# A planned order of instructions: forced first loads, slack ahead of the array, and local repacking

## The chip, the cores and the metric

The kernel runs on one core of a Trainium2 chip. The metric is the device time of one execution in microseconds (us); the kernel before takes 576.88 us, the median of three runs (576.75 to 577.52). Six queues issue instructions side by side and wait for each other by semaphores: PE (TensorE, the matmul array, with PEld for the loading of its weights), DVE (VectorE), ACT (ScalarE), POOL (GpSimd) and SP (SyncE, which here only starts DMAs).

## The reference

Two layers over x of 512 tokens by 1024 channels in float32. In each layer one projection `x @ w_in` (1024 by 3352) feeds three mixers side by side; the gated results go through one output projection and a LayerNorm.

```python
proj = x @ w_in
(rq, rk, rv, rg, nq, nkc, nvc, nks, nvs, nkw, nvw, ng, ngl, lx, lg) = jnp.split(proj, ...)
y_ret = retention(rq, rk, rv) * silu(rg)                    # 4 heads of 64, chunks of 128 tokens
y_nsa = nsa(nq, nkc, nvc, nks, nvs, nkw, nvw, ngl) * silu(ng)  # 8 heads; compressed, selected, window branch
y_lru = rg_lru(lx) * silu(lg)                               # convolution of width 4, gated scan
x = layer_norm(alpha * x + concat(y_ret, y_nsa, y_lru) @ w_out)
```

The NSA part makes softmax probabilities P for each tile of 128 tokens, group of 4 heads and branch, scales each by a gate over its sum, transposes them on PE and multiplies them with the values.

## The kernel before, in words

**Arithmetic.** Every product on PE keeps float32 accuracy by a split: an operand is written as a high part (`XH`, `wh`, `pth`) and a low part (`XL`, `wl`, `ptl`), and a product is three matmuls, high by high, high by low, low by high. ACT makes the high parts by a copy, DVE or POOL the low parts by a subtraction. So each weight that arrives by DMA in a raw buffer `wr` passes ACT (`wh`) and POOL or DVE (`wl`) before PE reads it, and each activation passes ACT (`XH`) and DVE (`XL`).

**Staging.** The activations stand as eight tiles of 128 channels by 512 tokens, `XH[:, k]`, `XL[:, k]`. The weights come in chunks of up to 280 columns, each in two halves of four k-tiles, by the function `weights` (line 563). There are two raw buffers `wr` and four buffers each of `wh` and `wl`. The order of the chunks is fixed: `nv` (the values and gates of NSA, 280 columns), `nk` (its keys, 256), `nq0`, `cmp`, `nq1`, and so on. In the first chunk of the first layer the loads are cut into single k-tiles, 140 KB of weights and 256 KB of x each, and x is loaded beside it (`load_x`, line 597; its buffer is `Y`). `proj_n` (line 611) has tokens as rows of the output, 3 matmuls of 280 columns for each k and token tile; `proj_t` (line 602) has 128 columns of the projection as rows and 512 tokens as columns. PSUM has banks A (three), S (two), M, T and O: `A` takes projections, `S` scores, `T` transposes, `O` the attention output.

**What sets the order.** Nothing is issued while the Python code runs. Every operation goes through `record` (line 201) into a `Plan` (line 287) with its engine, a cost in ns by formula (`Engine.cost`, line 244), and what it reads and writes. That is why all rows of the profile have one line, L208, or L239 for one group of matmuls (`together`, line 235); rows are told apart by the names of their tiles. `Plan.schedule` (line 353) then does list scheduling: `forward` (line 373) goes through model time and at each step issues, of the operations whose inputs are ready, the one that can start first, ties by priority. `lag` (line 348) is the model's delay from an operation to one that waits for it; rotating buffers are given out in recorded order. The first priorities are the longest remaining path plus noise from a random generator (`SEED`). `backward` schedules from the end, and up to six rounds of backward and forward keep the plan with the smallest model end. `emit` issues that plan; each engine then runs its instructions in that fixed order and only waits on semaphores. For the first chunk two of the weight loads are issued on ACT's queue (`W_ACT = 2`), the rest on SP's.

**The end.** `out_mm` and `out_norm` (lines 1087 and 1095) do the output projection in four chunks of 256 columns and the LayerNorm; at the end of layer 0 the four token tiles of `R` are normalised on DVE and POOL, transposed on PE through `T` (`T<-idr,R`, half a row of channels at a time) and split into the next layer's `XH` and `XL`.

Of the kernel before, what the change touches and what calls it, by code (L numbers as in the profile page):

```python
# [78 lines left out]
def _constants():  # L79
# [12 lines left out]
    for i in range(NT):  # L92
# [15 lines left out]
           ACT=dict(PE=281, DVE=152, ACT=148, POOL=170), POOL=dict(PE=203, DVE=60, ACT=75, POOL=100))  # L108
# [3 lines left out]
COLD = 6827.0  # L112
TURN = 130.0
GRAIN = 8
DMA_RATE = 360.0
BANKS = dict(A=3, M=1, S=2, T=1, O=1)
PBUFS = 7
WARM = 9
W_ACT = 2

NORM = [["AG", "AG", "VV", "VV"], ["AG", "AG", "VV", "VV"]]
LOCKS = True
HELD = 115.0
ACT_SOME = 0.0
POOL_EARLY = 60.0
K_ORDER = [0, 1, 6, 7, 2, 3, 4, 5]
# [3 lines left out]
SCALE = "GGGV"  # L130
W_ENG = "GGGG"
W_CUT = 2
SEED = 12
NOISE = 300.0
B_ATT = 50e3
B_LRU = 0.0
B_RET = 0.0
# [56 lines left out]
class Engine:  # L194
# [40 lines left out]
    def together(self, *products):  # L235

        def call():
            for out, lhsT, rhs, kw in products:
                self.queue.matmul(out.view(), lhsT.view(), rhs.view(), **kw)  # L239

        cost = 110.0 * len(products)
        self.plan.add(self.name, call, cost, [r for x in products for r in x[1:3]], [x[0] for x in products], None, False)

    def cost(self, what, args, kw):
        at = lambda x: x.view(0) if isinstance(x, Ref) else x
        size = lambda x: int(np.prod(x.shape[1:]))
        in_psum = lambda x: x.space == PSUM
        row = lambda x: x.offset // x.ap[0][0]
        out = at(args[0])
        n = size(out)  # L250
        if self.name == "SP":
            return max(475.0, out.nbytes() / DMA_RATE)
        if what == "dma_start":
            return 475.0
        if self.name == "PE":
            if what == "transpose":
                return 0.87 * at(args[1]).shape[0]
            m = size(at(args[1]))
            if at(args[2]).dtype == F32R:
                return max(0.4465 * n + 4.0, 0.86 * m)  # L260
            return max(1.8 * n, 1.73 * m)
        src = [at(x) for x in args[1:] if isinstance(x, Ref)]
        psum = any(in_psum(x) for x in src)
        moved = any(row(x) != row(out) for x in src)
        if self.name == "ACT":
            aps = any(isinstance(kw.get(k), Ref) for k in ("bias", "scale"))
            some = psum and src[0].shape[0] < P
            return (52 if psum else 93) + 0.833 * n + 93 * aps + 93 * ("accum_out" in kw) + 16 * moved + ACT_SOME * some
        n = max([n] + [size(x) for x in src])
        if self.name == "POOL":  # L270
            if kw.get("op") == ALU.pow:
                return 268 + 243.0 * n
            if what == "memset":
                return 60 + 0.5 * n
            return 230 + 0.863 * n if what == "tensor_scalar" else 120 + 2.2 * n
        if what == "reciprocal":
            return 60 + 6.3 * n
        if what == "tensor_tensor_scan":
            return 2.21 * n
        if what == "tensor_scalar" and "accum_out" in kw:  # L280
            return 190 + 1.042 * n
        if what in ("tensor_copy", "tensor_scalar", "memset") and not psum and not in_psum(out):
            return 67 + 0.521 * n + 62 * (len(src) - 1) + 93 * moved
        return 70 + 1.042 * n + 93 * moved + (8 if what == "tensor_tensor_reduce" else 0)


class Plan:
    ENGINES = ("PE", "DVE", "ACT", "POOL", "SP")

    def __init__(self, nc):  # L290
        self.ops, self.cells, self.bias = [], {}, 0.0
        queues = (nc.tensor, nc.vector, nc.scalar, nc.gpsimd, nc.sync)
        self.engines = [Engine(self, e, q) for e, q in zip(self.ENGINES, queues)]

# [15 lines left out]
        return self.cells[key]  # L310

    def add(self, eng, call, cost, reads, writes, table, lock, dma=False):
        op = Op(eng, call, cost, table, lock and LOCKS, len(self.ops))
        op.dma = dma
        for r in reads:
            q, m = self.touched(r)
            op.after.update(o for o, q2, m2 in r.buf.writes if q & q2 and m & m2)
        for r in writes:
            q, m = self.touched(r)
            op.after.update(o for o, q2, m2 in r.buf.writes + r.buf.reads if q & q2 and m & m2)  # L320
        for r in reads:
            r.buf.reads.append((op, *self.touched(r)))
        for r in writes:
            b, (q, m) = r.buf, self.touched(r)
            b.writes = [w for w in b.writes if w[1] & ~q or w[2] & ~m] + [(op, q, m)]
            b.reads = [w for w in b.reads if w[0] is op or w[1] & ~q or w[2] & ~m]
        op.after.discard(op)
        op.bufs = {r.buf for r in reads + writes}

        op.rows = {}  # L330
        if eng in ("ACT", "DVE") and not dma:
            for kind, refs in (("W", writes[:1]), ("R", reads)):
                for r in refs:
                    ap = r.view(0)
                    op.rows.setdefault((kind, ap.space == PSUM), ap.offset // ap.ap[0][0])
        for b in op.bufs:
            b.users += 1
        for o in op.after:
            o.before.append(op)
        op.bias = self.bias  # L340
        self.ops.append(op)
# [5 lines left out]
    @staticmethod  # L347
    def lag(a, b):
        if a.dma:
            return LAG_DMA  # L350
        return LAG[a.eng].get(b.eng, 150.0)

    def schedule(self):

        rank, noise = {}, NOISE * np.random.RandomState(SEED).standard_normal(len(self.ops))
        for op in reversed(self.ops):
            rank[op] = op.cost + max((self.lag(op, o) + rank[o] for o in op.before), default=0.0)
        self.end = self.forward({op: noise[op.ix] - rank[op] - op.bias for op in self.ops})
        best = self.end, {op: op.start for op in self.ops}
        for _ in range(ROUNDS):  # L360
            self.end = self.forward(self.backward())
            if self.end < best[0]:
                best = self.end, {op: op.start for op in self.ops}
        if best[0] < self.end:
            self.end = self.forward(best[1])
        return self.end

    @staticmethod
    def held(op, rows):
# [3 lines left out]
    def forward(self, prio):  # L373
# [16 lines left out]
        def place(op):  # L390
# [7 lines left out]
                t = max([t] + [end + TURN for e, end in b.seen.items() if e != op.eng])  # L398
            return t

        while len(self.order) < len(self.ops):
            best = None
            for e in ("POOL", "PE", "DVE", "ACT", "SP"):
                pick = None
                for op in ready[e]:
                    at = place(op)
                    if at is None:
                        continue
                    t = max(op.known, at, free[e] + self.held(op, rows), ports[e] if op.lock else 0.0)
                    k = (t, prio[op], op.ix)  # L410
                    if pick is None or k < pick[0]:
                        pick = k, op
                if pick and (best is None or pick[0][0] < best[0][0]):
                    best = pick
# [18 lines left out]
                ports["POOL"] = op.end  # L433
            ready[op.eng].remove(op)
            self.order.append(op)
            for b in op.bufs:
                b.last = max(b.last, op.end + self.release(op))
                if b.pool.turns and op.eng != "PE":
                    b.seen[op.eng] = op.end
                b.left -= 1  # L440
                if not b.left:
                    b.pool.free.append((b.last, b.slot))
# [57 lines left out]
def hybrid_kernel(ctx: ExitStack, tc: tile.TileContext, xt_d, xn_d, w_in_d, w_out_d, gb_d, cmpw_d, cmpp_d, lruw_d,  # L500
                  lrup_d, const_d, out_d):
    nc = tc.nc
    plan = Plan(nc)
# [59 lines left out]
    def weights(l, name):  # L563
        if (l, name) not in parts:
# [5 lines left out]
            for h in W_HALVES:  # L570
# [3 lines left out]
                lo = sb([P, 4, 280], "wl", WBUFS, F32R)[:, :, :n]  # L574
                if first:

                    for k in range(4):
                        u = slice(k, k + 1)
                        (A if 4 * h + k < W_ACT else Q).dma_start(raw[:, u, :], s3[:, r, :][:, u, :])
                        load_x(slice(4 * h + k, 4 * h + k + 1))  # L580
                        A.activation(hi[:, u], raw[:, u], AF.Copy)
                        (G if k % 2 else V).tensor_sub(lo[:, u], raw[:, u], hi.bitcast(F32)[:, u])
# [39 lines left out]
    for l in range(DEPTH):  # L622
# [1 line left out]

        vst = sb([P, NT, 2, 2, 2 * HD], "vst", dt=F32R)
        gate = sb([P, NT, 24], "gate")
        w = weights(l, "nv")
        pss = [bank("A") for _ in range(2)] + [bank("S") for _ in range(2)] if l == 0 else [None] * NT
        if l == 0:
            proj_n(w, [(i, ps[:, :280]) for i, ps in zip(TOKS, pss)], range(KT))  # L630
# [52 lines left out]

        kst = sb([P, 2, 2, 2 * S + 32], "K", dt=F32R)
        kf = kst.bitcast(F32)
        w = weights(l, "nk")
        for b in range(2):
            ps = bank("A")
            proj_t(w, b, ps)
            for g in range(2):  # L690
                me = slice(HD * g, HD * g + HD)
                ot = slice(HD * (1 - g), HD * (1 - g) + HD)
# [3 lines left out]
                def at(half, part, ap):  # L696
                    v = ap[half, g, part, c].rearrange("p (j t) -> p j t", j=NT)
                    return v if b else v[:, ::-1, :]
# [487 lines left out]
```

## Time and profile before

| what | value |
|---|---|
| median of three runs | 576.88 us |
| the profiled execution | 577.81 us, its span 576.0 us |
| mean granted TensorE clock | 0.992 of full speed |
| PE busy | 559.9 us (97%), 3718 instructions |
| DVE, ACT, POOL busy | 65%, 58%, 58% |
| DMA | 53.67 MB, mean 93 GB/s |

PE is busy for nearly the whole span, and the slowest of the others for two thirds of it. PE's rows overlap (a matmul is pipelined), so the duration of a matmul is longer than its distance to the next one: in one stretch matmuls of 512 columns that start at 36.60 and 36.83 have durations of 0.39 and 0.40. Idle time that a row gives in brackets stands just ahead of the row's start, with what ended it.

### The profile page before, as it was taken

The numbers are of one execution on the slowest core, as the hardware profiler recorded it, in microseconds if no ns is written. First come the engines' busy times: TensorE is split into PE (matmuls) and PEld (weight loads), VectorE is DVE, ScalarE is ACT, GpSimd is POOL, SyncE is SP. The second block draws the span as 40 slices with busy tenths as digits, with TensorE's granted clock in tenths as the row PEclk, the third lists the DMA queues.
The fourth block names the chain that finished last, engine by engine and source line by source line (L and its number), as shares of the span: only waits on it lengthen the run. The fifth ranks groups of instructions, "written<-read, shape, count | busy, mean of one in ns | idle before, by whom it ended". The sixth has DMA issues, their size and how long they took to land.

```text
span 576.0 us, 10627 instructions
## 1 busy us (share of the span) xinstructions
PE 559.9 (97%) x3718; PEld 500.6 (87%) x3718; DVE 373.8 (65%) x1113; ACT 331.6 (58%) x754; POOL 336.5 (58%) x512
## 2 busy tenths in 40 slices
PE   8999999999999999999989999999999999999994
PEld 7877888889998988899978788888988989889993
DVE  5660378898998754632873026877898886356257
ACT  6453578897775635611535238778967564454230
POOL 3753394377956348844763447633898273478442
PEclk8999999999999999999999999999999999999998
DMA  8743233020323036244253434211122122352303
GB/s 280 243 125 93 77 93 91 15 62 1 79 72 92 1 109 184 93 133 133 98 162 90 126 92 112 73 38 38 38 53 62 33 75 54 114 163 75 109 1 146
DMA packets 44789, 53.67 MB, mean 93 GB/s; under 512 B 3008, under 2 KB 37440, under 8 KB 44736
## 3 DMA queue, kind: packets, MB, share of 16 engines
q1 hardware_dynamic: 44448, 52.71, 31.0%
q8 instruction: 29, 0.48, 0.4%
q10 hardware_dynamic: 288, 0.29, 0.2%
q14 instruction: 24, 0.20, 0.1%
HBM read 47.75 MB, written 4.19 MB: 90 GB/s over the span
## 4 chain that ended last, share of the span: by engine, by line
PE 76%; DVE 9%; ACT 7%; DMA 4%; POOL 2%; issue 2%; DVEq 0%; POOLq 0%; ACTq 0%; SPq 0%
PE A L208 52%; PE T L208 6%; PE O L208 6%; PE S L208 5%; PE M L208 5%; DMA wr<-in_w_in_dram 3%; DVE R L208 2%; DVE P L208 2%; ACT P L208 1%; DVE Y L208 1%; ACT wh L208 1%; PE M L239 1%; DMA lp<-in_lrup_dram 1%; ACT pth L208 1%; POOL wl L208 1%
## 5 line engine op out<-in xcount | busy, mean ns | idle before, releaser
L208 POOL TENSOR_TENSOR wl<-wr,wh 128x256 fp32r<-128x256 f32 (+1 forms) x268 | 199.1, 771 | 114.1 <-ACT wh L208 107.2
L208 PE MATMUL A<-wh,XH 128*128 128x256 f32 (+1 forms) x560 | 154.2, 287 | 2.7 <-ACT wh L208 1.6
L208 PE MATMUL A<-wl,XH 128*128 128x256 f32 (+1 forms) x560 | 154.6, 286 | 0.0
L208 PE MATMUL A<-wh,XL 128*128 128x256 f32 (+1 forms) x560 | 153.5, 285 | 0.3 <-DVE XL L208 0.2
L208 ACT ACTIVATE wh<-wr 128x512 fp32r<-128x512 f32 (+2 forms) x140 | 81.7, 614 | 75.8 <-PE A L208 44.9
L208 PEld LDWEIGHTS A<-wh,XH 128*128 128x128 f32 x560 | 103.9, 189 | 6.3 <-ACT wh L208 1.8
L208 PEld LDWEIGHTS A<-wl,XH 128*128 128x128 f32 x560 | 104.7, 189 | 1.9
L208 PEld LDWEIGHTS A<-wh,XL 128*128 128x128 f32 x560 | 103.9, 189 | 2.6 <-DVE XL L208 0.7
L208 PE MATMUL A<-XH,wh 128*128 128x512 f32 x256 | 100.1, 401 | 0.2 <-DVE K L208 0.2
L208 PE MATMUL A<-XH,wl 128*128 128x512 f32 x256 | 100.1, 400 | 0.0
L208 PE MATMUL A<-XL,wh 128*128 128x512 f32 x256 | 99.2, 397 | 0.0
L208 POOL TENSOR_SCALAR P<-P,den,gate 128x256 f32<-128x256 f32 (+3 forms) x96 | 61.2, 651 | 40.8 <-DVE den L208 38.5
L208 ACT ACTIVATE P<-P,nmx 128x512 f32<-128x512 f32 (+3 forms) x128 | 70.8, 555 | 13.0 <-DVE nmx L208 12.7
L208 ACT ACTIVATE pth<-T 128x512 fp32r<-128x512 f32 x80 | 47.7, 596 | 43.6 <-PE T L208 36.6
L208 DVE TENSOR_TENSOR ptl<-T,pth 128x512 fp32r<-128x512 f32 x80 | 54.9, 686 | 22.1 <-ACT pth L208 21.1
L208 DVE CUSTOM_DVE_ANT_0 P<-S,con 128x512 f32<-128x512 f32 (+3 forms) x128 | 59.6, 484 | 12.9 <-PE S L208 7.4
L208 PE MATMUL S<-K,Q 128*128 128x288 f32 (+4 forms) x240 | 59.9, 340 | 0.3 <-DVE nmx L208 0.3
L208 PEld LDWEIGHTS A<-XH,wh 128*128 128x128 f32 x256 | 48.1, 188 | 10.3 <-issue 0.6
L208 PEld LDWEIGHTS A<-XH,wl 128*128 128x128 f32 x256 | 47.9, 188 | 9.6 <-POOL wl L208 0.5
L208 PEld LDWEIGHTS A<-XL,wh 128*128 128x128 f32 x256 | 48.1, 188 | 9.0
L208 PE MATMUL T<-idr,P 128*128 128x128 f32 x320 | 53.9, 275 | 1.9 <-DVE P L208 1.5
L208 PEld LDWEIGHTS T<-idr,P 128*128 128x128 f32 x320 | 38.4, 141 | 9.0 <-DVE P L208 2.0
(157 smaller groups left out, 860.6 us busy)
## 6 DMA issues: line engine op xcount, KB each, us to landing
wr<-in_w_in_dram SPq DMA_DIRECT2D x48, 512.0 KB, 3.8
wr<-in_w_out_dram SPq DMA_DIRECT2D x16, 512.0 KB, 3.8
Y<-in_xt_dram SPq DMA_DIRECT2D x8, 256.0 KB, 4.5
Y<-in_cmpw_dram SPq DMA_DIRECT2D x4, 512.0 KB, 5.9
R<-in_xn_dram SPq DMA_DIRECT2D x8, 256.0 KB, 3.4
P<-in_gb_dram SPq DMA_DIRECT2D x8, 256.0 KB, 3.9
x<-R SPq DMA_DIRECT2D x8, 256.0 KB, 2.1
R<-x SPq DMA_DIRECT2D x8, 256.0 KB, 3.6
```

Of the source, the lines that this page charges most:

```text
L208: return f(*[at(x) for x in args], **{k: at(v) for k, v in kw.items()})
L239: self.queue.matmul(out.view(), lhsT.view(), rhs.view(), **kw)
```

## The change

The computation is the same, operation for operation; the same 3557 matmuls are issued, and DVE and POOL get the same work. What changes is the planner, and through it the order on every engine, and the queue of two loads.

- Both first weight loads that stood on ACT's queue go to SP (`W_ACT` is gone).
- From the first load on until the weights of `nv` and `nk` are recorded, SP's DMAs are chained: the planner issues them in recorded order (`op.follows`). To that end `weights(l, "nk")` is recorded right after `weights(l, "nv")`.
- The model's cost of a DMA goes by 350 instead of 360 bytes per ns, and 200 for small rows or copies within one memory; the group of matmuls in `together` costs 121 instead of 110 ns each.
- `SLACK`: the planner's delay from another engine to PE is 200 ns longer than before.
- `SEED` is 9 instead of 12, and after the rounds of before, thirteen moves follow (`moved`): within a stretch of the plan around a random time the priorities get noise, the plan is packed anew forward, and backward and forward again up to twice; it stands if the model's end is smaller.

```diff
-DMA_RATE = 360.0
+DMA_RATE = 350.0
+DMA_SLOW = 200.0
-W_ACT = 2
+SLACK = 200.0
+PAD, PADDED = 0.0, ("DVE", "ACT", "POOL")
-SEED = 12
+SEED = 9
+MOVES = [4000, 4009, 4015, ...]
...
-        cost = 110.0 * len(products)
+        cost = 121.0 * len(products)
...
+            slow = size(out) * 4 < 2048 or at(args[1]).space == out.space
+            return max(475.0, out.nbytes() / (DMA_SLOW if slow else DMA_RATE))
...
+        if dma and eng == "SP" and self.chained is not None:
+            op.follows = self.chained[-1] if self.chained else None
+            self.chained.append(op)
...
-        return LAG[a.eng].get(b.eng, 150.0)
+        return LAG[a.eng].get(b.eng, 150.0) + (SLACK if b.eng == "PE" and a.eng != "PE" else 0.0)
...
-        if best[0] < self.end:
-            self.end = self.forward(best[1])
+        for move in MOVES:
+            best = self.moved(best, move)
+        self.end = self.forward(best[1])
...
+    def moved(self, best, move):
+        r = np.random.RandomState(move)
+        at, width, by = best[0] * r.rand(), 5e3 + 60e3 * r.rand() ** 2, 4e3 * r.rand() ** 2
+        noise = by * r.standard_normal(len(self.ops))
+        end = self.forward({op: t + (noise[op.ix] if abs(t - at) < width else 0.0) for op, t in best[1].items()})
+        got = end, {op: op.start for op in self.ops}
+        for _ in range(2):
+            self.end = got[0]
+            end = self.forward(self.backward())
+            if end >= got[0]:
+                break
+            got = end, {op: op.start for op in self.ops}
+        return got
...
+                    if op.follows and op.follows in waiting:
+                        continue
...
-                        (A if 4 * h + k < W_ACT else Q).dma_start(raw[:, u, :], s3[:, r, :][:, u, :])
+                        Q.dma_start(raw[:, u, :], s3[:, r, :][:, u, :])
...
-        w = weights(l, "nv")
+        w, w_keys = weights(l, "nv"), weights(l, "nk")
+        plan.chained = None
```

What this does to the order is seen at three places. First SP's queue from its start. Names: `wr` is a raw weight buffer (128x280 one k-tile of `nv`, 128x4x256 half of `nk`), `Y<-in_xt_dram` a k-tile of x, `con` constants. Before:

```order
L208 DMA Y_0_83<-in_xt_dram 128x512 x2
L208 DMA wr_0_86<-in_w_in_dram 128x280 x2
L208 DMA Y_0_83<-in_xt_dram 128x512 x4
L208 DMA wr_1_87<-in_w_in_dram 128x280
L208 DMA Y_0_83<-in_xt_dram 128x512
L208 DMA wr_0_86<-in_w_in_dram 128x4x256
L208 DMA wr_1_87<-in_w_in_dram 128x280 x3
L208 DMA Y_0_83<-in_xt_dram 128x512
L208 DMA con_0_65<-in_const_dram 128x1457
```

Of the change, from its second half of `nv` on (the first eight rows alternate in the same way on `wr_0`):

```order
L211 DMA wr_1_87<-in_w_in_dram 128x280
L211 DMA Y_0_83<-in_xt_dram 128x512
L211 DMA wr_1_87<-in_w_in_dram 128x280
L211 DMA Y_0_83<-in_xt_dram 128x512
L211 DMA wr_1_87<-in_w_in_dram 128x280
L211 DMA Y_0_83<-in_xt_dram 128x512
L211 DMA wr_1_87<-in_w_in_dram 128x280
L211 DMA Y_0_83<-in_xt_dram 128x512
L211 DMA wr_0_86<-in_w_in_dram 128x4x256
L211 DMA con_0_65<-in_const_dram 128x1457
L211 DMA wr_1_87<-in_w_in_dram 128x4x256
```

The pairs of w and x now alternate from the first to the eighth, both halves of `nk` stand behind all of x, and only the constants stand between those halves. Before, six of x were ahead of the fifth w on this queue, and the first half of `nk` was ahead of the last x.

Second, PE where layer 1 begins: `nv` of one token tile in bank `A`, and the transposes of the last tile (`R_6`) of layer 0. Before:

```order
L208 MATMUL A_2_98<-wh_2_90,XL_0_82 128x280
L208 MATMUL A_2_98<-wh_2_90,XH_0_81 128x280
L208 MATMUL A_2_98<-wl_2_94,XH_0_81 128x280
L208 MATMUL A_2_98<-wh_2_90,XL_0_82 128x280
L208 MATMUL T_0_79<-idr_0_66,R_6_73 128x128 x4
L208 MATMUL A_0_96<-wh_0_88,XH_0_81 128x280
L208 MATMUL A_1_97<-XH_0_81,wh_3_91 128x512
L208 MATMUL A_0_96<-wl_0_92,XH_0_81 128x280
```

Of the change:

```order
L211 MATMUL A_2_98<-wl_0_92,XH_0_81 128x280
L211 MATMUL T_0_79<-idr_0_66,R_6_73 128x128 x4
L211 MATMUL A_2_98<-wh_0_88,XL_0_82 128x280
L211 MATMUL A_2_98<-wh_1_89,XH_0_81 128x280
L211 MATMUL A_2_98<-wl_1_93,XH_0_81 128x280
L211 MATMUL A_2_98<-wh_1_89,XL_0_82 128x280
L211 MATMUL A_2_98<-wh_1_89,XH_0_81 128x280
L211 MATMUL A_2_98<-wl_1_93,XH_0_81 128x280
L211 MATMUL A_2_98<-wh_1_89,XL_0_82 128x280
L211 MATMUL A_1_97<-wh_0_88,XH_0_81 128x280
L211 MATMUL A_0_96<-XH_0_81,wh_2_90 128x512
```

Seven matmuls of the tile before now stand between the transposes and the first matmul that reads what is made of them; before there was none.

Third, DVE in layer 1 around the scaling of probabilities of 128 columns (token tile 0, second group of heads), in `scale_row` with the reciprocals `den_2` and `den_3`. Before:

```order
L208 ISA P_2_131,nmx_0_124<-S_0_99,con_0_65 128x512
L208 ISA nmx_0_124 128x1
L208 TENSOR_SCALAR P_6_135<-P_6_135,den_2_122,gate_0_85 128x128
L208 TENSOR_TENSOR denc_1_139<-denc_1_139,gate_0_85 128x4
L208 TENSOR_TENSOR ptl_0_143<-T_0_79,pth_0_141 128x512
L208 TENSOR_SCALAR P_6_135<-P_6_135,den_3_123,gate_0_85 128x128
```

Of the change:

```order
L211 ISA P_1_130,nmx_0_124<-S_0_99,con_0_65 128x512
L211 ISA nmx_0_124 128x1
L211 RECIPROCAL den_2_122<-den_2_122 128x4
L211 TENSOR_SCALAR P_6_135<-P_6_135,den_2_122,gate_0_85 128x128
L211 TENSOR_REDUCE denc_1_139<-pcm_0_128 128x4
L211 RECIPROCAL den_3_123<-den_3_123 128x4
L211 RECIPROCAL denc_1_139<-denc_1_139 128x4
L211 TENSOR_SCALAR P_6_135<-P_6_135,den_3_123,gate_0_85 128x128
```

The two scalings now follow their reciprocals directly and stand one behind the other; before, the low part `ptl` of the transposes stood between them.

## Rows read from the trace of the kernel before

**Rows 1.** Busy time by stretch: engine busy (x instructions), PE's granted clock, DMA share, GB/s.

```profile
0.00:11.00 11.00, 8.31 (x40) 7.98 (x41) 5.86 (x12) 6.80 (x13) 3.59 (x12) 0.84 0.80 254
...
280.00:300.00 20.00, 18.30 (x140) 17.17 (x139) 17.06 (x31) 9.47 (x21) 17.45 (x20) 1.00 0.43 135
...
560.00:576.00 16.00, 7.57 (x65) 7.36 (x63) 12.24 (x25) 1.22 (x2) 4.98 (x4) 0.83 0.35 132
sum 576.00, PE 559.94 PEld 500.58 DVE 373.76 ACT 331.59 POOL 336.53; mean PE 55.99 PEld 50.06 DVE 37.38 ACT 33.16 POOL 33.65
```

**Rows 2.** Waits of PE: total us, times, longest us.

```profile
PE A L208 <- ACT wh L208: 1.6, 1, 1.6
PE T L208 <- DVE P L208: 1.5, 2, 1.3
PE A L208 <- ACT XH L208: 0.9, 2, 0.7
```

**Rows 3.** Timeline of the start: start us, duration us, engine, operation, [idle before].

```profile
0.72 0.89 ACTq L208 DMA_DIRECT2D wr<-in_w_in_dram  x2
...
0.72 0.86 SPq L208 DMA_DIRECT2D Y<-in_xt_dram  x2
...
4.73 0.44 ACT L208 ACTIVATE wh<-wr 128x280 fp32r<-128x280 f32 x1 [1.81 <-DMA wr<-in_w_in_dram]
5.08 0.61 ACT L208 ACTIVATE XH<-Y 128x512 fp32r<-128x512 f32 x1
```

**Rows 4.** Timeline where PE works through `nk`, 36 to 38 us.

```profile
36.60 0.39 PE L208 MATMUL A<-XH,wh 128*128 128x512 f32 x1
...
36.83 0.40 PE L208 MATMUL A<-XL,wh 128*128 128x512 f32 x1
37.35 1.15 ACT L208 ACTIVATE wh<-wr 128x512 fp32r<-128x512 f32 x2
...
37.43 0.50 PE L208 MATMUL A<-XH,wh 128*128 128x512 f32 x1 [0.20 <-DVE K L208]
```

**Rows 5.** Timeline where layer 1 begins, 288 to 300 us.

```profile
288.23 1.28 POOL L208 TENSOR_TENSOR lwl<-R,lwh 128x512 fp32r<-128x512 f32 x1
288.25 1.80 DVE L208 SCALAR_TENSOR_TENSOR R<-R,rs,P 128x512 f32<-128x512 f32 x1
...
290.11 0.66 PE L208 MATMUL T<-idr,R 128*128 128x128 f32 x4 [0.64 <-DVE R L208]
...
295.52 0.39 PE L208 MATMUL A<-wh,XL 128*128 128x280 f32 x1 [0.20 <-DVE XL L208]
...
296.00 0.29 PE L208 MATMUL A<-wh,XL 128*128 128x280 f32 x1
...
296.13 0.29 PE L208 MATMUL A<-wh,XH 128*128 128x280 f32 x1
...
297.88 0.39 ACT L208 ACTIVATE vst<-A 128x256 fp32r<-128x256 f32 x1 [2.94 <-PE A L208]
298.16 0.18 ACT L208 ACTIVATE gate<-A 128x24 f32<-128x24 f32 x1
...
298.98 0.40 PE L208 MATMUL A<-wh,XH 128*128 128x280 f32 x1 [0.69 <-ACT XH L208]
```

**Rows 6.** Timeline of the third place of the change, 440 to 445 us.

```profile
440.08 1.31 POOL L208 TENSOR_SCALAR P<-P,den,gate 128x128 f32<-128x128 f32 x3
...
440.82 2.45 DVE L208 TENSOR_SCALAR P<-P,den,gate 128x128 f32<-128x128 f32 x1
...
443.33 0.33 PE L208 MATMUL T<-idr,P 128*128 128x128 f32 x1 [1.34 <-DVE P L208]
...
444.99 0.34 DVE L208 TENSOR_SCALAR P<-P,den,gate 128x128 f32<-128x128 f32 x1
```

**Rows 7.** Timeline of the end.

```profile
567.36 0.72 DVE L208 SCALAR_TENSOR_TENSOR R<-R,rs,P 128x512 f32<-128x512 f32 x1
568.01 0.40 DVE L208 SCALAR_TENSOR_TENSOR R<-R,A 128x256 f32<-128x256 f32 x1
```

More of the change, by code (lines that the diff above doesn't have):

```diff
@@ L132 @@
 W_CUT = 2
-SEED = 12
+SEED = 9
 NOISE = 300.0
+MOVES = [4000, 4009, 4015, 4016, 4029, 4031, 4037, 4062, 4071, 4076, 4079, 4094, 4103]
 B_ATT = 50e3
@@ L251, in cost @@
         if self.name == "SP":
-            return max(475.0, out.nbytes() / DMA_RATE)
+            slow = size(out) * 4 < 2048 or at(args[1]).space == out.space
+            return max(475.0, out.nbytes() / (DMA_SLOW if slow else DMA_RATE))
         if what == "dma_start":
@@ L291, in __init__ @@
         self.ops, self.cells, self.bias = [], {}, 0.0
+        self.chained = None
         queues = (nc.tensor, nc.vector, nc.scalar, nc.gpsimd, nc.sync)
@@ L312, in add @@
     def add(self, eng, call, cost, reads, writes, table, lock, dma=False):
-        op = Op(eng, call, cost, table, lock and LOCKS, len(self.ops))
-        op.dma = dma
+        op = Op(eng, call, cost + PAD * (eng in PADDED), table, lock and LOCKS, len(self.ops))
+        op.dma, op.follows = dma, None
+        if dma and eng == "SP" and self.chained is not None:
+            op.follows = self.chained[-1] if self.chained else None
+            self.chained.append(op)
         for r in reads:
@@ L399, in place @@
             return t
+        waiting = {op.follows for op in self.ops if op.follows}
         while len(self.order) < len(self.ops):
@@ L435, in forward @@
             self.order.append(op)
+            waiting.discard(op)
             for b in op.bufs:
@@ L575, in weights @@
                 if first:
+                    plan.chained = plan.chained or []
                     for k in range(4):
                         u = slice(k, k + 1)
-                        (A if 4 * h + k < W_ACT else Q).dma_start(raw[:, u, :], s3[:, r, :][:, u, :])
+                        Q.dma_start(raw[:, u, :], s3[:, r, :][:, u, :])
                         load_x(slice(4 * h + k, 4 * h + k + 1))
@@ L685, in hybrid_kernel @@
         kf = kst.bitcast(F32)
-        w = weights(l, "nk")
         for b in range(2):
             ps = bank("A")
-            proj_t(w, b, ps)
+            proj_t(w_keys, b, ps)
             for g in range(2):
```

## The prediction, made before the changed kernel was run

> **What bounds the kernel now.** I read the busy time by stretch first. PE is busy for 559.94 of 576.00 us, so 16.06 us are idle [rows 1]. Of these 2.69 lie in the first 11 us, before the first operands are there, and 8.43 in the last 16 (16.00 less 7.57): the last matmul ends at 567.57 and what follows is the last LayerNorm and the store. That leaves 16.06 - 2.69 - 8.43 = 4.94 us in all the stretches between. PE's work itself is not changed: the same matmuls of the same sizes. So the change can win only from 16 us, and a planner's order mainly from the 4.94. Second come the waits of PE, for what these are [rows 2]: one long wait for the first weights, which is the start, one of 1.3 us for DVE's probabilities, two for `XH` that make 0.9, and a few of some tenths. The timelines give their places [rows 4 to 6].
>
> An idle gap costs a little more than it shows. The row at 36.83 is followed by one at 37.43, where matmuls of 512 columns else start 0.23 apart (36.60 to 36.83) [rows 4]. The step is 0.60 instead of 0.23, so a shown wait of 0.20 costs 0.37, which is 0.17 more. There are about ten such waits between the start and the end, so what could be recovered there is 4.94 + 10 x 0.17 = 6.6 us. No order can win more than this in the middle.
>
> **The start.** Before, the first weight and the first x are issued at the same moment, 0.72, on two queues [rows 3]. The first weight's copy on ACT starts at 4.73 and that of x at 5.08. Now both stand on SP, and an issue takes 0.86 / 2 = 0.43 there [rows 3]. Two answers bound this. If the bytes decide the landing, the first pair (140 and 256 KB) has the engines for itself instead of sharing them with a second pair; x can then be copied as soon as the weight's 0.44 on ACT is over, and up to 0.35 (5.08 - 4.73) is won. If the issue decides, x comes 0.43 later and all of PE with it. I take a gain of 0.2, since both w and x must be there for the first matmul and the pair now comes first together; both ends stay in the range. The Trainium skill, "DMA: Bandwidth & Descriptors", section "Issuing engines are not separate DMA queues", says that DMAs issued by several engines run on the same 16 engines, and that spreading them saves only issue time. By that rule alone this move could only lose, 0.4 us, and the sum below would be 0.6 higher; the two rows at 0.72 agree that an issue costs about as much on either queue, and no row of before shows the pair on one queue.
>
> After that the supply of `nv` should hold: x and w alternate, and all of x lies ahead of `nk`.
>
> **The step from `nv` to `nk`.** PE now does all of `nv` first, where before it put the first half of `nk` between. Behind `nv` ACT has four evictions of 0.39 and four gates of 0.18 to do [rows 5], 2.3 us, and in its order the last conversion of `nk`, two copies of together 1.15 [rows 4], stands behind them: 3.4, and with some 0.2 for the hand-overs (an estimate, the size of the small waits in rows 5) 3.65. PE has by then 13 matmuls of the first half of `nk` at 0.23, 3.0. So PE waits some 0.6, and the wait of 0.37 at 37.43 [rows 4] belongs to the work that has moved and goes: +0.3 after rounding up. Bounds: 0, if the first evictions begin before `nv` has ended, and +2.3, if all eight small operations come in a row with no matmul beside them.
>
> **The scaling of the probabilities.** At 440.82 the scaling of one 128x128 tile on DVE takes 2.45 us, where the same form takes 0.34 at 444.99 [rows 6]. POOL works through three scalings from 440.08 to 441.39 and further work after that without a pause. PE waits 1.34 for it [rows 6], a cost of 1.34 + 0.17 = 1.5. In the new order the scaling stands right behind its reciprocal, another reciprocal's scaling beside it, and POOL has at that place only scalings of P, none of the `wl` subtractions that followed before. I take it that this wait goes: -1.5. The bounds are -1.5 and what the second rival says.
>
> **The boundary of the layers.** The stretch 280 to 300 has 1.70 us of idle PE [rows 1], in four waits: 0.64 for `R` from DVE, 0.69 for `XH`, 0.20 for `XL` and the rest, 0.17, for `XH` [rows 2, 5]. They cost 1.70 + 4 x 0.17 = 2.4. Seven matmuls now stand between the last transposes and the first that reads `XH`; at a distance of 0.13 (296.00 to 296.13) [rows 5] that is 0.9 us of work, against none before, and ACT's copy behind the transposes has to fit into it. It covers the wait of 0.69. The wait of 0.64 came from a DVE operation of 1.80 beside one of POOL that began 0.02 earlier [rows 5]; the new order does not clearly part these two. One of the transposes has gained in distance, another has lost. I take half: -1.2, with bounds -2.4 and 0.
>
> **The rest.** Of the 6.6 us these places hold 1.5, 2.4 and 0.4; 2.3 are left in small waits. With 200 ns more of planned distance to PE, the shortest distance from the transposes to the first value matmul grows by some tenths in the new order, but not at all places: the distance at which the bank T is used again shrinks. Half of it, -1.2; bounds -2.3 and +1.0, the last if as many small waits appear as go (four of 0.1 to 0.2 more than before).
>
> **The end.** After the last matmul's own addition (0.40 at 568.01 [rows 7]) DVE has one more normalising step than before, 0.66 by the distance from 567.36 to 568.01 (with the overlap) [rows 7], because the order puts it behind; but that addition can begin some 0.4 earlier for it. +0.2, bounds -0.4 and +0.7.
>
> **The sum.** -0.2 + 0.3 - 1.5 - 1.2 - 1.2 + 0.2 = -3.6. Against the profiled execution, 577.81 us with a span of 576.0 (1.8 lie outside the span), this is 574.2; the median of the runs is 0.93 below that execution, 576.88, and against it the forecast is 573.3. Under 0.2%, 1.15 us, a difference can't be told from none.
>
> **Rivals.**
>
> First, the waits only move. The order is planned with fixed durations, but what makes the waits are operations that take three or seven times as long as usual when DVE and POOL meet (1.80 and 2.45 [rows 5, 6]). For it: the same two engines have the same work, so they meet as often, elsewhere. Against it: all waits on PE through the middle together are only 4.94, and a meeting costs only where PE has no spare matmuls. Then only the start and a fragment of the rest count: 576.88 - 0.4, about 576.5.
>
> Second, the meeting comes back at the same place and is worse. In the new order the scores of that token tile stand nearer to the transposes of its probabilities: between them PE has 3.0 us of other matmuls, where it had 5.7 (those that stand between in the two orders, each by the distance that its form has in the trace, as 0.23 for 512 columns and 0.13 for 280). If DVE's scaling there again takes 2.45, the wait is not 1.5 but 1.5 + 2.7 = 4.2, and the sum is -3.6 + 1.5 + 4.2 = +2.1: 579.0. It decides from the point where POOL's scalings begin before DVE's and follow each other without a gap. For it: the row at 440.82 begins 0.74 after POOL's [rows 6], and three scalings of POOL stand beside two of DVE now too. Against it: POOL's later subtractions are gone from there, so the block lasts at most what is left of 1.31. The Trainium skill, "SBUF — State Buffer", section "SBUF: two separate sides", calls the port pair that DVE and GpSimd share an exclusive lock: whichever starts first holds it for its whole instruction and the other fully blocks. The trace agrees, with 2.45 beside 0.34 for one form; it is what this rival needs, and by it alone a DVE operation could be let in between two of POOL's.
>
> Third, nearly all of the middle goes: the slack was what was missing. Then it is 6.6 from the middle, and the start gives another 0.35 and up to 1 from a better filled first stretch, where PE's granted clock is 0.84 in the mean against 1.00 later [rows 1], which over 11 us is 1.8 us of full-speed work not had: 576.88 - 6.6 - 0.35 - 1.0 = 568.9. For it: every one of the waits shown is shorter than 1.4. Against it: the slack is 0.2 and several waits exceed it.
>
> **How the numbers follow.** The forecast 573.3 has a chance of 0.62, and by the bounds of its terms a range of its own of 571 to 575.5. The first rival has 0.16 (576.5), the second 0.10 (579.0), the third 0.12 (568.9). The range of 8 in 10 takes in the third's centre and most of the second: 569.0 to 578.3. Faster by over 0.2% (under 575.7): all of the third, nearly all of the forecast, a quarter of the first, 0.12 + 0.61 + 0.04 = 0.77. Slower (over 578.0): the second and a little of the first, 0.11. Within: 0.12.
>
> **What would show it.** In the profile of the changed kernel, PE's row for the scalings of P in layer 1 has no wait over 0.5 and no DVE scaling of 128x128 takes over 1 us there; the stretch around the boundary has under 1 us of idle PE, and the first matmul behind the last transposes starts without a wait for `XH`; between `nv` and `nk` there is one wait of about 0.6 for `wh`; ACT's first copy of x starts within 0.4 us of 5.08; and the last matmul ends near 564, with about 8.6 us behind it. The forecast is wrong if PE's idle time between the start and its last matmul stays over 4 us, or if one wait over 2 us appears.

## The result and the profile after

The changed kernel takes 573.45 us, the median of four runs (572.88 to 574.24), against 576.98 for the kernel before (576.75 to 577.52): a ratio of 0.9938, with a 95% interval of 0.9921 to 0.9956. Run again later it gave 573.02 (six runs) and a ratio of 0.9936 [0.9913, 0.9959]. So it is 3.5 us faster; the forecast was 3.6.

The two profiled executions are further apart than the medians. Before's was one of its longer ones (577.81 us, span 576.0), that of the change its shortest (572.88, span 571.1): 4.9 us. All of it lies ahead of PE's last matmul, which ends at 562.53 instead of 567.57.

The busy time by stretch of the changed kernel, in the columns of [rows 1]:

```profile
0.00:11.00 11.00, 9.96 (x60) 9.96 (x61) 5.49 (x11) 7.10 (x13) 3.77 (x13) 1.00 0.80 261
...
120.00:220.00 100.00, 97.28 (x703) 89.49 (x702) 83.04 (x278) 66.35 (x163) 63.88 (x99) 1.00 0.24 70
280.00:300.00 20.00, 19.80 (x146) 18.56 (x145) 17.68 (x34) 8.66 (x19) 16.21 (x17) 1.00 0.49 155
300.00:400.00 100.00, 98.42 (x548) 81.98 (x546) 51.16 (x152) 62.69 (x142) 51.15 (x76) 1.00 0.29 81
400.00:480.00 80.00, 79.84 (x599) 75.18 (x599) 68.47 (x236) 59.58 (x150) 53.96 (x85) 1.00 0.21 57
```

And the kernel before, in the two stretches that the forecast had no rows for:

```profile
120.00:220.00 100.00, 99.53 (x720) 91.37 (x719) 82.51 (x286) 69.39 (x169) 62.51 (x99) 1.00 0.22 63
300.00:400.00 100.00, 100.00 (x561) 83.58 (x561) 52.51 (x158) 62.38 (x143) 49.81 (x77) 1.00 0.32 87
```

The first row holds the surprise: by 11 us PE has issued 60 matmuls instead of 40, at a granted clock of 1.00 instead of 0.84. The boundary, 280 to 300, is down from 1.70 to 0.20 us of idle PE. But 120 to 220 has risen from 0.47 to 2.72 and 300 to 400 from nothing to 1.58. The waits of PE say what they are:

```profile
PE T L211 <- DVE ptl L211: 2.7, 1, 2.7
PE T L242 <- DMA Y<-Y: 1.0, 1, 1.0
...
PE A L211 <- DVE K L211: 0.5, 1, 0.5
PE A L211 <- DVE XL L211: 0.4, 2, 0.2
PE T L211 <- POOL P L211: 0.2, 1, 0.2
```

Of the waits in [rows 2], that for `wh` at the start, those for `XH` at the boundary and the long one for `P` are gone; the last two were forecast. One new wait is longer than any of them. Its place in the timeline, POOL, DVE and PE side by side:

```profile
211.17 4.16 POOL L211 TENSOR_TENSOR wl<-wr,wh 128x256 fp32r<-128x256 f32 x6
...
211.62 3.73 DVE L211 TENSOR_TENSOR rrs<-rrs,con 128x4 f32<-128x4 f32 x1
...
215.38 0.69 DVE L211 TENSOR_TENSOR ptl<-T,pth 128x512 fp32r<-128x512 f32 x1
...
216.13 0.66 PE L211 MATMUL T<-idr,P 128*128 128x128 f32 x4 [2.71 <-DVE ptl L211]
```

`rrs` is a product of 128x4 numbers whose median over eight is 0.16 us. Beside six subtractions of POOL without a pause it takes 3.73 and ends when they do; the low part `ptl` stands behind it on DVE, and PE's transposes into bank T behind that.

The start, to be read beside [rows 3]:

```profile
0.72 0.38 SPq L211 DMA_DIRECT2D wr<-in_w_in_dram  x1
...
1.16 0.42 SPq L211 DMA_DIRECT2D Y<-in_xt_dram  x1
...
2.93 0.44 ACT L211 ACTIVATE wh<-wr 128x280 fp32r<-128x280 f32 x1 [0.93 <-DMA wr<-in_w_in_dram]
...
3.94 0.63 ACT L211 ACTIVATE XH<-Y 128x512 fp32r<-128x512 f32 x1 [0.57 <-DMA Y<-in_xt_dram]
...
4.90 0.58 PE L211 MATMUL A<-wh,XH 128*128 128x280 f32 x1
```

The first weight is copied at 2.93 instead of 4.73 and x at 3.94 instead of 5.08, so the first pair does land earlier when it is issued ahead of the others. PE starts on `nv` at 4.90, against 6.16 before. Not all of this is the landing. The plan of before loads the k-tiles in an order of its own, which the names of the buffers don't show: with the number of the k-tile it is x0 x1 | w1 w0 on ACT's queue | w3 w2 x6 x2 x3 x4 w4 x5, half of `nk`, w6 w5 w7 x7. So the row at 4.73 in [rows 3] is w1, and PE's first matmul, which reads w0, waits for the second copy:

```profile
5.67 0.44 ACT L208 ACTIVATE wh<-wr 128x280 fp32r<-128x280 f32 x1
...
6.16 0.53 PE L208 MATMUL A<-wh,XH 128*128 128x280 f32 x2 [1.65 <-ACT wh L208]
```

For the comparison of all runs one measure is used below. PE's work is the same in all of them, so for each matmul the distance to the next one is taken, less the median distance of its form in before's profile; the sum of these differences over a stretch is what PE **lost** there. The start is the time of the first matmul of `nv` plus what is lost up to 40 us; the middle is what is lost from 40 us to the last matmul. In the two profiles above the start falls from 8.7 to 5.8 and the middle from 14.1 to 11.9; how the distances are grouped moves these values by up to 0.4.

### The profile page after: what moved, and what is told of

The parts are those of the page before. It is cut to its first block, busy times and chain, and to the rows that moved or that the text cites. A ratio compares the mean times of both kernels' runs of the same rounds, so it can differ in the third digit from the quotient of the medians.

```text
span 571.1 us, 10615 instructions
## 1 busy us (share of the span) xinstructions
PE 556.5 (97%) x3718; PEld 500.7 (88%) x3718; DVE 375.1 (66%) x1113; ACT 332.0 (58%) x754; POOL 338.8 (59%) x512
## 4 chain that ended last, share of the span: by engine, by line
PE 92%; DVE 4%; ACT 1%; DMA 1%; issue 1%; POOL 0%; DVEq 0%; ACTq 0%; POOLq 0%
PE A L211 62%; PE S L211 8%; PE T L211 8%; PE O L211 7%; PE M L211 5%; DMA Y<-Y 1%; DVE K L211 1%; DVE XL L211 1%; PE M L242 1%; PE T L242 1%; DVE rrs L211 1%; DVE R L211 1%; DVE ptl L211 1%; ACT K L211 1%; POOL P L211 0%
## 5 line engine op out<-in xcount | busy, mean ns | idle before, releaser
L211 PE MATMUL A<-wh,XL 128*128 128x256 f32 (+1 forms) x560 | 151.0, 285 | 0.4 <-DVE XL L211 0.4
L211 PEld LDWEIGHTS A<-wh,XL 128*128 128x128 f32 x560 | 102.7, 189 | 2.4 <-DVE XL L211 0.8
L211 PE MATMUL A<-XL,wh 128*128 128x512 f32 x256 | 101.1, 401 | 0.0
L211 PE MATMUL A<-XH,wl 128*128 128x512 f32 x256 | 98.7, 398 | 0.0
L211 POOL TENSOR_SCALAR P<-P,den,gate 128x256 f32<-128x256 f32 (+3 forms) x96 | 64.2, 681 | 44.9 <-DVE den L211 31.4
L211 ACT ACTIVATE P<-P,nmx 128x256 f32<-128x256 f32 (+3 forms) x128 | 71.1, 556 | 19.4 <-DVE nmx L211 18.5
L211 DVE CUSTOM_DVE_ANT_0 P<-S,con 128x256 f32<-128x256 f32 (+3 forms) x128 | 59.9, 483 | 9.1 <-PE S L211 5.8
L211 PE MATMUL T<-idr,P 128*128 128x128 f32 x320 | 55.6, 274 | 2.9 <-DVE ptl L211 2.7
```

Of the source, the lines that this page charges most:

```text
L211: return f(*[at(x) for x in args], **{k: at(v) for k, v in kw.items()})
```

## Experiments

Unless they say "planned anew", the experiments keep the planned order of one kernel on every engine and move only what is named.

**The loads alone (b_start), and the old loads in the new order (a_start).**

```diff
 # b_start: the sixteen first loads of before
-x0 x1 | w1 w0 on ACT's queue | w3 w2 x6 x2 x3 x4 w4 x5 [nk] w6 w5 w7 x7
+w0 x0 w1 x1 w2 x2 w3 x3 w4 x4 w5 x5 w6 x6 w7 x7 [nk], all on SP
 # a_start: on the change; queues and pattern of before, k-tiles in rising order
-w0 x0 w1 x1 w2 x2 w3 x3 w4 x4 w5 x5 w6 x6 w7 x7 [nk], all on SP
+x0 x1 | w0 w1 on ACT's queue | w2 w3 x2 x3 x4 x5 w4 x6 w5 w6 w7 x7 [nk]
```

> The order of before on every engine, but with the sixteen first loads (eight of w, eight of x) in the order of the change, alternately and all on SP. Theory: the start is worth 2.7 us (in the two traces the first real matmul begins 1.26 earlier and 1.40 less is lost up to 11 us), so 576.9 - 2.7 = 574.2, less what the first half of nk loses by standing behind all of x (up to 1). Rival, the forecast's own split: the start is worth 0.2, so 576.7.

> The order of the change on every engine, but with the sixteen first loads in the order of before: x, x on SP beside w, w on ACT's queue, then w, w, four x and so on. Theory, the start is worth 2.7 us: 573.4 + 2.7 = 576.1, and the first real matmul at 6.1 us. Rival, the start is worth 0.2: 573.6.

b_start took 581.15 us, 1.0062 of before [1.004, 1.0084]: slower, which neither theory had. a_start took 574.01, 0.9939 [0.9916, 0.9963], the same as the change. So both the forecast's "the loads are worth 0.2" and the theory "the loads are worth 2.7" miss something. In b_start the loads come in the order of the k-tiles, but ACT keeps before's order of copies, and its third copy of x is that of x6, now the seventh to be loaded. ACT stands idle until x6 has landed at 12.12, though x2 was there at 7.79; PE, whose next matmuls need x2, waits behind it:

```profile
12.14 2.19 ACT L208 ACTIVATE XH<-Y 128x512 fp32r<-128x512 f32 x4 [3.18 <-DMA Y<-in_xt_dram]
```

```profile
5.70 0.52 PE L208 MATMUL A<-wh,XH 128*128 128x280 f32 x2 [1.25 <-ACT wh L208]
13.35 0.52 PE L208 MATMUL A<-wh,XH 128*128 128x280 f32 x2 [1.56 <-ACT XH L208]
15.72 0.53 PE L208 MATMUL A<-wl,XH 128*128 128x280 f32 x2 [0.43 <-DVE wl L208]
```

Start 11.4, against 8.7 before: the loads come in an order that the copies don't follow. So b_start prices a mismatch, not the new loads. In a_start PE begins `nv` only at 5.96, but loses 0.1 up to 40 us; start 6.0, against 5.8 for the change. What an early first matmul wins is lost again by waiting, in small steps, for what comes behind it. Before's own order of the k-tiles was not tried in the new plan.

**Half of nk ahead of the last three w and the last x (a_nk).**

```diff
 # on a_start
-... w4 x6 w5 w6 w7 x7 [nk]
+... w4 x6 [nk] w5 w6 w7 x7
```

> The order of the change on every engine, but SP's first loads exactly as before, with the first half of nk ahead of the last three w and the last x. Theory, what counts is that no load of nk stands ahead of what nv needs while PE does all of nv first: x7 lands some 2 us later, PE waits for its XH, +1 to +2 against the change, 575. Rival, PE's own order (all of nv first) carries the gain and has slack: under +0.5, 573.9.

575.24 us, 0.9981 [0.9964, 0.9998]. x7 lands at 15.21 instead of 12.18, but PE does not wait for it. It waits 0.46 at 13.80 for the XH of x5, which landed at 8.95 but whose copy stands on ACT behind that of w5; and w5, also behind the half of `nk` now, lands at 12.77; the start is 6.7. The interval lies above those of the change and of a_start; the step has the size that the first theory wanted, 1.2 us over a_start and 1.8 over the change, but not by the wait that it named. Its profile gives the start 0.7 of this; its middle was also 1.8 longer than that of a_start, above all from 300 to 400 us, where nothing was edited.

**A shorter gap ahead of the first matmul (b_warm).**

```diff
-for i in range(9):    # zero matmuls: eight ahead of the first real one, one behind
+for i in range(12):   # all ahead
```

> Before with twelve instead of eight zero matmuls ahead of the first real one, so that PE has no gap between 4.51 and 6.16 us; loads and all else as before. Theory, the gap holds the clock at its lower level: full clock from about 6.5 instead of 10.8 us, so half of some 4 us is won, 1.5 to 2 us, 575.1. Rival, the arrival of the operands alone decides: no change, 576.9.

578.07 us, 1.0012 [0.9996, 1.0028]: no gain. PE's wait ahead of its first real matmul was 0.35 us instead of 1.65, and the clock stayed at 1.00 in this profile, which is of the shortest of the twelve runs (576.02). It stayed there too in the profile of b_lock, whose start is that of before to the last instruction and has a gap of 1.22. Here are 7.4 to 10.6 us of before and then of b_lock:

```profile
7.40:10.60 3.20, 3.20 (x16) 3.20 (x16) 3.20 (x6) 2.50 (x5) 0.78 (x1) 0.51 0.88 270
```

```profile
7.40:10.60 3.20, 3.20 (x27) 3.16 (x26) 3.20 (x6) 2.64 (x6) 0.71 (x1) 1.00 0.89 269
```

At the lower level PE does 16 matmuls and at the higher 27 in the same time, yet the start is 8.7 in the one and 8.1 in the other: at the higher clock PE runs into a wait for `wl` (0.85 at 17.71; in b_warm 0.64) that the profile of before does not have. The low clock in the profile of before was one draw and cost 0.6, and a rare one: its mean clock is 0.992, and of 63 timed runs of before taken beside the experiments only two show that, the others 0.994 to 0.997. So there was nearly nothing for b_warm to win.

**The meeting at 441 us of before (b_lock).**

```diff
 # POOL, behind the three scalings of P with den_3
-R<-rt, wl, wl, pcm
+pcm, R<-rt, wl, wl
```

> Before with one change on POOL at 441 us: the compressed branch's product (pcm), which waits for DVE, is put ahead of one gather step (R) and two subtractions (wl), so POOL pauses after its three scalings. Theory, DVE's scaling waits for a pause of POOL: it takes under 1.1 us instead of 2.45, PE's wait of 1.34 goes, 576.9 - 1.5 = 575.4. Rival, the long scaling has another reason (or the wait moves to wl, 0.5 us later): 2.4 us again and 576.9 or a little more.

In it part of the output differs: the next load into the raw buffer `wr` is issued at 437.25 instead of 442.53 and lands at 441.00, ahead of a moved subtraction `wl` that still reads that buffer. The work is the same. It took 577.05 us, 0.9988 [0.9974, 1.0002]: the scaling took 0.34 and PE's long wait is gone, but the median did not fall. What speaks for the rival is b_warm, where the order at this place is that of before, untouched:

```profile
439.62 1.40 POOL L208 TENSOR_SCALAR P<-P,den,gate 128x128 f32<-128x128 f32 x3
...
440.36 0.34 DVE L208 TENSOR_SCALAR P<-P,den,gate 128x128 f32<-128x128 f32 x1
```

DVE's scaling begins 0.74 after POOL's, as in [rows 6], and takes 0.34 instead of 2.45. In b_start's profile it took 2.43 again, also 0.74 behind. Three profiles of one order at this place, two of them with the meeting: DVE gets in between POOL's operations in one execution and not in another, and how often is not known. So b_lock's 0.34 need not come from its edit, and the forecast's 1.5 us was the price of one draw.

**The meeting at 211 us of the change (a_ptl).**

```diff
 # DVE
-rrs, ptl, ryn x2, ptl, ryn x2, ptl
+ptl, ptl, rrs, ryn x4, ptl
```

> The order of the change, but on DVE the small product rrs with con (128x4, 3.73 us long beside six subtractions of POOL at 211 us) and the four ryn behind it are put behind the next two low parts ptl. Theory, this meeting of DVE and POOL costs the wait of 2.7 us at 216.13: it goes, 573.5 - 2.9 = 570.6; a part of it may come back where ryn is needed at 217.4. Rival, as at 441 us before: the wait of one profile is the draw of one execution, and the median falls by under 1 us.

570.0 us (568.85 to 571.58), 0.9886 [0.9866, 0.9905]: the fastest of all, 3.4 us under the change (3.0 under the change run again) and 6.7 under before. `rrs` now meets POOL's last subtraction only:

```profile
214.56 0.69 DVE L211 TENSOR_TENSOR ptl<-T,pth 128x512 fp32r<-128x512 f32 x1 [1.60 <-ACT pth L211]
215.17 0.28 DVE L211 TENSOR_TENSOR rrs<-rrs,con 128x4 f32<-128x4 f32 x1
```

This meeting was no draw in any profile of the order. In a_start, a_nk and the change run again, `rrs` took 3.74, 3.73 and 3.73 us and PE waited 2.70 or 2.71: `rrs` begins 0.45 behind the start of the first of six equal operations without a pause, and does not get in before the last has ended. Not every operation of DVE is held there. In a_ptl the six subtractions run from 211.22 to 215.43, and the low part at 214.56, which reads `T` in PSUM and `pth` in SBUF, takes its usual 0.69 beside them; `rrs` reads two tiles in SBUF.

**The change again (a_again), without the moves (r_moves0), without the slack (r_slack0), the last two planned anew.**

```diff
 # r_moves0
-MOVES = [4000, 4009, 4015, ...]
+MOVES = []
 # r_slack0
-SLACK = 200.0
+SLACK = 0.0
```

> The change itself once more, to see which of its waits are in every execution. Theory: the long product rrs (3.7 us) and PE's wait of 2.7 at the same place are there again, since they stand in three profiles of this order; the wait for Y<-Y (1.0 in one profile, 0 and 0.5 in two others) is a draw; the median stays at 573.5 within 0.5. Rival: the 3.7 us is a draw too, and half of the waits are elsewhere.

> The change without its thirteen moves, planned anew: chained loads, slack, new costs and seed 9 stay. Its PE order begins as that of the change (92 matmuls of nv, then nk). Theory, the start's 2.4 us stay and the middle is another draw of 10 to 13 us of losses: 573 to 576. Rival, the moves carry the gain: 577 or more.

> The change with a slack of 0 instead of 200 ns, planned anew with all else of the change. Its PE order begins with 95 matmuls of nv, then nk. Theory, the start's 2.4 us stay; the middle loses more small waits (0.1 to 0.4 us each) than with slack, and meetings of DVE and POOL as before: 574 to 577. Rival, slack does nothing that can be measured: 573.5 within 0.5.

a_again: as theory had it, with the wait of 2.7 and only 0.1 for `Y<-Y`. r_moves0: 575.12 us, 0.9976 [0.9961, 0.9992]; `rrs` takes at most 1.26 there, but PE waits 2.9 once for XH at 237.82, and the middle is 12.5 against 11.9 and 11.4 for the change. r_slack0: 593.92, 1.0298 [1.0265, 1.0331], far outside both expectations. Its waits:

```profile
PE M L211 <- POOL ryn L211: 3.8, 1, 3.8
PE A L211 <- ACT XH L211: 3.3, 3, 1.6
PE A L211 <- DVE K L211: 2.9, 1, 2.9
PE O L211 <- ACT pth L211: 1.0, 1, 1.0
```

The middle is 33.5. Five waits of over 1 us make up 11 of it. Around them the granted clock falls four times (last section), and with these come many small ones. The moves were chosen with slack in place, so this plan is not the best that can be had without it; that slack of 200 ns is worth 20 us is not shown, only that this plan without it is that much worse.

**Each half alone, planned anew (r_chain, r_rest).**

```diff
 # r_chain: on the change
-DMA_RATE = 350.0; DMA_SLOW = 200.0; SLACK = 200.0; SEED = 9; MOVES = [...]; cost = 121.0
+DMA_RATE = 360.0; DMA_SLOW = 360.0; SLACK = 0.0; SEED = 12; MOVES = []; cost = 110.0
 # r_rest: on the change
-plan.chained = plan.chained or []
+plan.chained = None     # and two loads on ACT's queue, nk recorded late
```

> One half of the change alone, planned anew: the chained first loads on SP with the weights of nk recorded early; costs, seed, slack and moves as before. Its PE order has nk behind 68 matmuls of nv instead of 60. Theory, the start carries 2.3 us of the 3.5: 574.7, with one us either way for the new order of the rest. Rival, the forecast's split, the start nothing and the middle 3.9: 577.

> The other half alone, planned anew: slack of 200 ns, the new costs, seed and thirteen moves; the loads unchained, two of w on ACT's queue, nk recorded late. Its PE order begins nk behind 60 matmuls of nv, as before. Theory, 1.3 us of the 3.5: 575.7, with one us either way. Rival, the forecast's split: 573.1.

r_chain took 582.1 us, 1.0096 [1.0069, 1.0123], and r_rest 576.59, 1.0 [0.9981, 1.0019]. Neither half brings the gain. In r_chain the loads are those of the change, but PE has 28 of the 96 matmuls of `nv` behind some of `nk`; its start is 7.8, and the plan has long waits for `ryn` and `ptl` (middle 19.5). In r_rest the middle is 11.9, as in the change, but the start 9.1, as before. Together they are 3.5 us faster. What the two do only together is to put 92 of the 96 matmuls of `nv` ahead of `nk`; it is 68 in r_chain and 60 in r_rest and before. The start goes with that count: 8.1 to 9.1 with 60 (before, b_warm, b_lock, r_rest), 7.8 with 68, and 5.8 to 6.9 with 92 or more (the change, a_start, a_nk, r_moves0, r_slack0); b_start, with 60 and its copies out of step, is at 11.4. That the count is the cause is argued: no run moves it alone.

## Why the prediction came out right, and where its working did not

Time, sign and range held. The split did not; from the two profiles, by loss (the end by the span behind the last matmul):

| term | forecast | measured |
|---|---|---|
| the start, to 11 us | -0.2 (-0.35 to +0.43) | -2.7: 1.26 by the first matmul, 1.4 by loss |
| `nv` to `nk`, 11 to 40 | +0.3 (0 to +2.3) | -0.2 |
| scaling of P at 441 | -1.5 | -1.5 |
| boundary, 280 to 300 | -1.2 (-2.4 to 0) | -1.9 |
| the rest of the middle | -1.2 (-2.3 to +1.0) | +1.2 |
| the end | +0.2 (-0.4 to +0.7) | +0.1 |

The measured terms add up to -5.0, the distance of the two profiles, where the forecast's add up to -3.6 and the medians are 3.5 apart.

**The start** was mis-sized, and beyond its bounds. The step "both ends stay in the range" took the arrival of the first pair for all that the start holds, and took w1 for the weight of that pair. It left out that before loses 2.5 us between its first matmul and 40 us: to a half clock in its own profile, to a wait for `wl` (0.85 and 0.64 us) in others of the same order. The idle rows hide this, since a PE at half clock is busy. The runs put the cause on the match of orders, not on the queues. With before's order on ACT and PE, loads in the new order cost 4 us (b_start); with the new order on both, loads on before's queues and in before's pattern cost nothing that can be measured, as long as `nk` stays behind them (a_start), and 1.2 us more where it doesn't (a_nk). The forecast named this ("all of x lies ahead of `nk`") and gave it no price; it also took "all of `nv` first" for a small term, where nearly all of `nv` first goes with the shorter start.

**The step from `nv` to `nk`** had a wait of 0.6 for `wh`; there is no such wait, and the lower bound 0 was nearer. **The scaling** went as forecast in the profiles, but the runs show that its wait was there in only some executions, so that in the medians the term can be smaller than 1.5. **The boundary** gave more than forecast, within its bounds: seven matmuls of work do cover XH, and the wait of 0.64 for `R`, which the forecast left open, is gone too. This held in every profile: PE loses 0.9 there in all five of the new order and 2.2 to 3.6 in the four of before's. **The rest** has the wrong sign. The second rival, a meeting of DVE and POOL with a wait of over 2 us, came true, at 211 us instead of 441; its mechanism was right, its price 2.7 instead of 4.2 and its place wrong, and the forecast had looked for it only where before had shown one. The stretch 300 to 400 lost 2.4 more as well, of which the wait for `Y<-Y` is 1.0. **The end** was right.

So the number came out partly by luck: 2.5 us more at the start and 2.4 less in the rest nearly cancel, and the 1.4 by which the measured terms exceed the forecast's are what before's profile lies above its median and the change's below (0.8 and 0.6). By the forecast's own criterion, "PE's idle time between the start and its last matmul stays over 4 us", it was wrong: it is 4.97, where it was 4.94, and one wait of over 2 us did appear. ACT's first copy of x came 1.14 us earlier, not within the 0.4 that was to show the start right. In the working, one reading of its own numbers was off: the range 569.0 to 578.3 leaves out the centres of the second rival (579.0) and, by 0.1, of the third (568.9).

What stays open: how much of the gain each part of the planner's change carries, since any edit of it gives another plan with other meetings, and the plans that were tried differ by far more (573 to 594 us) than the effect looked for. That the start and the boundary are where the time was won is read from profiles; no run takes one of them away from the change alone.

## What to carry to other kernels

Price the start of a pipelined kernel by the work done at some later time (matmuls issued by 40 us), not by idle time or by the first instruction: an order of loads is worth something only together with the order in which they are copied and used. Compare orders by what is loaded, not by the name of the buffer alone. A wait read from one profile is one draw where two engines meet by chance; look at the same place in a second execution before pricing it. After a new schedule, search the trace for short operations that take many times their median beside a block of another engine without a pause; moving one such operation and the four behind it won 3.0 to 3.4 us here, nearly as much as the whole change.

## What the runs showed of the hardware

Ahead of PE's last matmul its granted clock fell from 1.00 to 0.50, the lower of its two levels (1.2 instead of 2.4 GHz), only around waits of PE: during a wait or up to 1.6 us after its end. These were waits of 1.65 us at the start of before, of 1.25 there in b_start, of 2.70 and 2.71 up to 216.59 us in a_start and 216.98 in a_nk, of 2.93 up to 237.82 in r_moves0, of 1.64 and 1.14 up to 524.95 in r_chain, and four times in r_slack0. Other waits of such sizes, 1.22 at the start of b_lock, 1.96 at 428.84 in r_chain and 2.71 in both profiles of the change, had no such fall behind them. Two stretches behind the same wait, a_start and then a_again:

```profile
217.40:220.80 3.40, 3.40 (x11) 2.61 (x10) 1.14 (x3) 1.38 (x3) 1.67 (x3) 0.51 0.45 145
```

```profile
216.60:220.00 3.40, 3.40 (x20) 2.87 (x21) 1.41 (x5) 2.08 (x4) 0.97 (x2) 1.00 0.52 154
```

11 matmuls against 20 in 3.4 us. From 210 to 225 us PE lost 4.5 and 4.6 us in a_start and a_nk, 3.0 and 2.9 in the two profiles of the change, and 0.7 in a_ptl, which has no wait there. So the fall cost 1.6 us beyond the wait, in some executions; that would fit the 3.0 to 3.4 us that a_ptl won by taking away 2.7, but which of the timed runs had a fall at this place isn't recorded.

The copy `Y<-Y` at 331 us, from one SBUF tile to itself, landed 5.11 us after its issue in the profile of the change and 3.14 after it before, with two weight loads of 512 KB issued 0.7 and 1.7 later in both; PE's wait for it was 1.0, 0.5, 0.5 and twice 0.1 us in five profiles of the same order.
